# DeltaNet mixer of a two-layer decoder step: logits by float32 products in column groups, first decays spread by TensorE, gate and output products between the steps of the block inverse

## The chip, the cores and the metric

The kernel runs on one core of a Trainium2 chip. The metric is device time in microseconds of one execution. The core's engines run side by side and meet at semaphores: PE (TensorE, products into PSUM), DVE (VectorE), ACT (ScalarE), POOL (GpSimd) and SP (SyncE, which here issues the transfers).

## The reference, cut to what matters

Two macaron layers act on 544 tokens (a prompt of 512 and a sample group of 8 x 4) with 1024 channels. A layer is a feed-forward half step, a mixer, and another feed-forward half step. The change is in the mixer of the second layer, a gated DeltaNet with 8 heads of 128 channels:

```python
def deltanet_mixer(u, conv_buf, S0, w_in, conv_w, A_log, dt_bias, o_gain, w_out):
    proj = u @ w_in
    qkv, z, b_logit, a_logit = jnp.split(proj, [3 * DN_WIDTH, 4 * DN_WIDTH, 4 * DN_WIDTH + DN_HEADS], axis=-1)
    qkv, new_buf = causal_conv(conv_buf, qkv, conv_w)
    ...
    beta = jax.nn.sigmoid(b_logit.astype(jnp.float32))
    g = -jnp.exp(A_log.astype(jnp.float32)) * jax.nn.softplus(a_logit.astype(jnp.float32) + dt_bias.astype(jnp.float32))
    o, S = gated_delta_chunked(q, k, v, beta, g, S0)
    o = rms_norm(o, o_gain) * jax.nn.silu(z.reshape(B, T, DN_HEADS, DN_HEAD_DIM).astype(jnp.float32))
    return o.reshape(B, T, DN_WIDTH).astype(u.dtype) @ w_out, (new_buf, S)
...
def gated_delta_chunked(q, k, v, beta, g, S0):
    G = jnp.cumsum(gc, axis=-1)
    decay = jnp.exp(jnp.where(incl, G[..., :, None] - G[..., None, :], -jnp.inf))
    A = jnp.where(strict, jnp.einsum('bnhcd,bnhsd->bnhcs', kc, kc) * decay, 0.0) * bc[..., None]
    sol = lax.linalg.triangular_solve(A, rhs, left_side=True, lower=True, unit_diagonal=True)
    ...
    def step(S, xs):
        U = uv - jnp.einsum('bhcd,bhde->bhce', wk, S)
        O = jnp.einsum('bhcd,bhde->bhce', qq, S) + jnp.einsum('bhcs,bhse->bhce', p, U)
        S = gg[..., None, None] * S + jnp.einsum('bhcd,bhce->bhde', kk, U)
```

## The kernel before, in words

Tokens lie along the free dimension: each of the 8 tiles `x` holds 128 channels of all 544 tokens, in two halves of 256 and 288 columns. A large product (`mm3`, L371 to L373) keeps float32 accuracy by splitting both sides in a high and a low part (`xh`, `xl`; `wh`, `wl`) and multiplying three times per 128 channels: 24 matmuls for a half, 48 for a weight tile of 128 output channels, into PSUM buffers called `lin`. Its weights come by a DMA (`raw`), and ACT (L332) and DVE (L333) split them.

The mixer works on pairs of heads, called groups 0, 2, 4 and 6 by their first head. `ODD_ORDER` lists its pieces in the order in which they are written: D (decays of a pair), H (q and k of a head, convolution, k k^T and q k^T), B (values), V (the diagonal 32x32 blocks of the triangular solve, 31 small steps on DVE at L1257 and L1258, with transfers through DRAM that end in `V<-tdr`), L (`levels`, which builds the inverse of the 128x128 blocks from the 32x32 ones), S (the sample group), C (`chain`, the recurrence over four chunks, and `finish`, which normalizes and gates the outputs `y`), R (sample state), Z (gate of a head), O and M (output product of one group, or of groups 2 and 4 together), N (convolution state). Within this, a list scheduler sets the final order on every engine from its own estimates; each engine then runs its instructions strictly in that order.

`odd_setup` comes first: the 16 logits per token as an `mm3` product with a 16 columns wide weight (`lin` with 128\*16 weights in the trace), scaled by `rstd` into `bt` (L1049), turned by transposes (L1053), then beta, g, the cumulative sums `G` (L1076 to L1080), and its transpose `gt`, which goes to DRAM (`gdr`). A DMA spreads each head's row over all partitions (`grow` or `xsq`, and `grs` for the sample), and 8 DVE instructions a head (L1171, L1172) form the decays `Dn` and `Dt`.

In `levels` all small products (L1282 to L1309) use one PSUM slot, "c", and each step's result is evacuated by DVE and ACT before the next: transposes `pt`, `py`, `pz` (24 matmuls), a second `py`, a second `pz`. What the scheduler finds ready runs on PE between these steps. The `chain` of the last group calls `finish` after chunk 2 and after chunk 4, and the output product of group 6 takes the first half of the tokens first, in tiles of 6 matmuls.

The constants of the mixer are loaded by `odd_consts` at the start of the feed-forward step ahead of it, and `E.junk` is a tile that takes the unwanted output of ACT's squares.

## Time and profile before

| | |
|---|---|
| median of 3 runs | 1913.84 us (1910.95 to 1916.3) |
| the profiled execution | 1910.86 us, of which 1909.1 us from the first to the last instruction |
| mean granted clock of TensorE | 0.991 |
| PE, DVE, ACT busy | 97%, 57%, 44% of the span |
| the mixer, 1189 to 1610 us | PE 399.23, DVE 341.82, ACT 255.49 of 421.00 us, clock 0.97 |

The trace gives each instruction a start and a length; the idle time of its engine before it and what ended that idle time stand in brackets. Matmuls are pipelined, so the pace of a run of them is the distance of their starts. The granted clock of a window is a mean between the two levels of TensorE's clock, 1.2 GHz (0.50) and 2.4 GHz (1.00).

### The profile page before, as it was taken

To read this page: it belongs to the slowest core of one execution; us is meant where nothing else is said; L and a number is where in the kernel's file an instruction comes from. 1 tells how busy PE (TensorE), PEld (TensorE's weight loads), DVE (VectorE), ACT (ScalarE), POOL (GpSimd) and SP (SyncE) were. 2 spreads that over 40 slices of the span, in tenths; PEclk is the share of its full clock that TensorE was granted. 3 is DMA by queue.
4 is the path that set the end of the run, shared out by engine and by line. 5 is a ranking of instruction groups with operands and counts; after the bars stand their busy time and mean duration, and the time that the engine had idled before them with its cause. 6 is when DMAs were issued, how large, how long until landed. Compare 5 with 4: busy or idle time off the path is not lost.

```text
span 1909.1 us, 36695 instructions
## 1 busy us (share of the span) xinstructions
PE 1860.2 (97%) x15101; PEld 1790.8 (94%) x15101; DVE 1078.9 (57%) x2565; ACT 836.2 (44%) x1733; POOL 123.6 (6%) x229
## 2 busy tenths in 40 slices
PE   7999999999999999999999999999999998999999
PEld 6999999889778999999999999899888988999998
DVE  7444434786866444434444433898878867444422
ACT  6333224777755333323333322566675636333221
POOL 0000001111430000000000000212111100000000
PEclk8999999999999999999999999999999999999999
DMA  4333333312432333223333322334333332333242
GB/s 128 86 88 89 89 89 89 90 57 80 138 100 69 89 89 89 82 86 101 87 88 88 93 86 75 88 98 113 82 102 88 95 90 59 89 89 88 78 112 69
DMA packets 315973, 171.05 MB, mean 90 GB/s; under 512 B 28470, under 2 KB 310278, under 8 KB 315804
## 3 DMA queue, kind: packets, MB, share of 16 engines
q1 hardware_dynamic: 313244, 160.30, 29.6%
q0 software_dynamic: 2560, 8.39, 1.5%
q8 instruction: 119, 1.95, 0.4%
...
## 4 chain that ended last, share of the span: by engine, by line
PE 59%; DVE 4%; ACT 3%; DMA 1%; issue 1%; SPq 0%; ACTq 0%; DVEq 0%
PE lin L371 18%; PE lin L373 18%; PE lin L372 18%; PE m L1217 0%; DMA raw<-in_w_in_odd 0%; DMA raw<-in_w_ffn_in 0%; DVE acc L1140 0%; DVE wl L333 0%; DVE LT L1258 0%; PE c L1355 0%; PE c L1323 0%; DMA S<-in_state_dn_S 0%; DVE ltmp L1257 0%; PE c L1309 0%; PE c L1304 0%
## 5 line engine op out<-in xcount | busy, mean ns | idle before, releaser
L371 PE MATMUL lin<-xh,wh 128*128 128x256 f32 (+2 forms) x2992 | 873.0, 292 | 12.2 <-DVE x L1594 4.2
L372 PE MATMUL lin<-xl,wh 128*128 128x256 f32 (+2 forms) x2992 | 868.1, 290 | 0.7 <-DVE xl L273 0.6
L373 PE MATMUL lin<-xh,wl 128*128 128x256 f32 (+2 forms) x2992 | 865.6, 290 | 1.5 <-DVE wl L333 1.5
L371 PEld LDWEIGHTS lin<-xh,wh 128*128 128x128 f32 (+1 forms) x2992 | 563.9, 189 | 18.7 <-DVE x L1594 4.2
L373 PEld LDWEIGHTS lin<-xh,wl 128*128 128x128 f32 (+1 forms) x2992 | 565.3, 189 | 3.7 <-DVE wl L333 1.9
L372 PEld LDWEIGHTS lin<-xl,wh 128*128 128x128 f32 (+1 forms) x2992 | 564.2, 189 | 2.7 <-DVE xl L273 1.5
L332 ACT ACTIVATE wh<-raw 128x1024 fp32r<-128x1024 f32 x261 | 275.6, 1057 | 494.9 <-PE lin L372 429.4
L333 DVE TENSOR_TENSOR wl<-raw,wh 128x1024 fp32r<-128x1024 f32 x261 | 317.6, 1217 | 89.9 <-PE lin L373 88.0
L371 PE MATMUL lin<-hh,wh 128*128 128x288 f32 (+1 forms) x1024 | 295.7, 289 | 0.0
L372 PE MATMUL lin<-hl,wh 128*128 128x288 f32 (+1 forms) x1024 | 295.4, 288 | 0.0
L373 PE MATMUL lin<-hh,wl 128*128 128x288 f32 (+1 forms) x1024 | 294.9, 288 | 0.0
L372 PEld LDWEIGHTS lin<-hl,wh 128*128 128x128 f32 x1024 | 193.0, 188 | 0.2
L373 PEld LDWEIGHTS lin<-hh,wl 128*128 128x128 f32 x1024 | 192.7, 188 | 0.1
L371 PEld LDWEIGHTS lin<-hh,wh 128*128 128x128 f32 x1024 | 192.5, 188 | 0.1
L410 DVE TENSOR_TENSOR sg<-lin,rstd 128x256 f32<-128x256 f32 (+1 forms) x128 | 56.1, 438 | 162.5 <-PE lin L373 162.3
L415 DVE TENSOR_TENSOR pr<-lin,rstd 128x256 f32<-128x256 f32 (+1 forms) x128 | 56.5, 441 | 155.2 <-PE lin L373 155.2
L379 ACT ACTIVATE hh<-pr 128x256 fp32r<-128x256 f32 (+1 forms) x128 | 55.1, 431 | 202.8 <-DVE pr L416 202.6
L432 DVE SCALAR_TENSOR_TENSOR x<-lin,x 128x256 f32<-128x256 f32 x64 | 28.2, 441 | 168.4 <-PE lin L373 168.4
L380 DVE TENSOR_TENSOR hl<-pr,hh 128x256 fp32r<-128x256 f32 (+1 forms) x128 | 56.6, 442 | 61.2 <-ACT hh L379 61.2
L100 ACT ACTIVATE sg<-sg 128x256 f32<-128x256 f32 (+1 forms) x128 | 53.9, 422 | 56.1 <-DVE sg L410 56.1
L272 ACT ACTIVATE xh<-x,vec 128x544 fp32r<-128x544 f32 (+2 forms) x64 | 39.6, 632 | 71.8 <-DVE x L432 59.6
L1140 DVE SCALAR_TENSOR_TENSOR acc<-XP,cw,acc 128x568 f32<-128x568 f32 x72 | 58.7, 818 | 2.5 <-ACT acc L1138 1.8
...
## 6 DMA issues: line engine op xcount, KB each, us to landing
raw<-in_w_ffn_in SPq DMA_DIRECT2D x128, 512.0 KB
...
```

Of the source, the lines that this page charges most:

```text
L100: i = self.nc.scalar.activation(out, in_, func, **kw).ins
L272: nc.scalar.activation(xh, x, AF.Copy, scale=g)
L332: nc.scalar.activation(self.h, raw, AF.Copy)
L333: nc.vector.tensor_tensor(self.l, raw, self.h.bitcast(F32), op=ALU.subtract)
L371: nc.tensor.matmul(ps[:n], lhsT=wh, rhs=rh, start=(i == 0), stop=False)
L372: nc.tensor.matmul(ps[:n], lhsT=wh, rhs=rl, start=False, stop=False)
L373: E.last_mm = nc.tensor.matmul(ps[:n], lhsT=wl, rhs=rh, start=False, stop=(i == len(terms) - 1)).ins
L379: nc.scalar.activation(yh, src, AF.Copy)
L380: nc.vector.tensor_tensor(yl, src, yh.bitcast(F32), op=ALU.subtract)
L410: nc.vector.tensor_tensor(s, ps, E.rstd[:, c0:c0 + cn], op=ALU.mult)
L415: nc.vector.tensor_tensor(p_, ps, E.rstd[:, c0:c0 + cn], op=ALU.mult)
L1140: nc.vector.scalar_tensor_tensor(a, XP[:, j:j + XW - 3], cw[j], a, op0=ALU.mult, op1=ALU.add)
```

## The change

The logits. `odd_consts` now loads the 1024x16 logit weights into `bw`, zero-padded to 32 columns, and DVE multiplies them by the norm's gains, all at the start of the feed-forward step ahead of the mixer. `odd_setup` multiplies them with the raw float32 tiles `x`, in 16 matmuls that put four channel tiles in four groups of 32 output partitions; `rstd` scales the result, and a float32 product with `bsum` (four stacked identities) adds the groups where the transposes were. The logits have to follow the norm's own products (`E.norm_mm`). Three constants are loaded later, in `odd_setup`.

The first decays. For heads 0 and 1 and for the sample, matmuls with a broadcast column of the identity spread the rows of `gt` over all partitions into PSUM, and DVE reads them there; the other heads still use the DMA.

The fill. Gate products of heads 0 to 3, half of O0 and M2 in quarters leave `ODD_ORDER` and are called inside `levels`, one piece after each of its first four steps; each later step on PE has to stand behind the last matmul of the piece before it. M2 is then split in m-tiles 0 to 3 (fill) and 4 to 7. The four pieces of O0 cover all of it.

The unwanted squares go to `kt`, `vb` and `kw` in place of `junk`.

```diff
-ODD_ORDER = "D0 H0 H1 B0 B1 V0 Z0 L0 Z1 S0 C0 R0 D2 H2 B2 H3 B3 Z2 Z3 V2 L2 D4 S2 C2 R2 H4 H5 B5 D6 Z4 B4 V4 Z5 H6 S4 H7 B6 L4 V6 C4 R4 B7 Z6 O0 Z7 S6 N L6 C6 R6 M2 O6"
+ODD_ORDER = "D0 H0 H1 B0 B1 V0 L0 S0 C0 R0 D2 H2 B2 H3 B3 V2 L2 D4 S2 C2 R2 H4 H5 B5 D6 Z4 B4 V4 Z5 H6 S4 H7 B6 L4 V6 C4 R4 B7 Z6 Z7 S6 N L6 C6 R6 M2 O6"
+FILL = {0: ("Z00", "Z01", "Z10", "Z11"), 2: ("Z20", "Z21", "Z30", "Z31"), 4: ("O002", "O022", "O042", "O062"),
+        6: ("M201", "M211", "M221", "M231")}
...
+    E.bw = op.tile([P, KD, 32], F32, name="bw")
+    nc.vector.memset(E.bw, 0.0)
+    nc.sync.dma_start(out=E.bw[:, :, :16], in_=w_in[:, 4096:4112].rearrange("(k p) c -> p k c", p=P))
+    for k in range(KD):
+        nc.vector.tensor_scalar(E.bw[:, k], E.bw[:, k], col(E, "norm_mix", KD + k), None, op0=ALU.mult)
...
-    w = W(E, w_in[:, 4096:4112])
...
-    mm3(E, [w], E.xh, E.xl, ev)
+    for (c0, cn), tag in zip(HALVES, ("z", "pv")):
+        ps = cps(E, [P, cn], tag)
+        for i in range(2):
+            for j in range(4):
+                mm = nc.tensor.matmul(ps[32 * j:32 * j + 32], lhsT=E.bw[:, 4 * i + j], rhs=E.x[4 * i + j][:, c0:c0 + cn], start=(i == 0), stop=(i == 1), skip_group_check=True)
+                E.after(mm.ins, E.norm_mm)
+        nc.vector.tensor_tensor(bt[:, c0:c0 + cn], ps, E.rstd[:, c0:c0 + cn], op=ALU.mult)
...
-        nc.tensor.transpose(ps[:n, t], bt[:16, c0:c0 + n], E.ident[:16, :16])
+        nc.tensor.matmul(ps[:n, t], lhsT=bt[:, c0:c0 + n], rhs=E.bsum, start=True, stop=True)
...
-    nc.sync.dma_start(out=E.grs, in_=E.gdr[:, T:].unsqueeze(0).to_broadcast([P, NH, NS]))
+    row = lambda r: E.ident[:40, r:r + 1].to_broadcast([40, P])
+    ps = cps(E, [P, NH, NS], "s")
+    for h in range(NH):
+        nc.tensor.matmul(ps[:, h], lhsT=row(32 + h), rhs=gt[:40, :NS], start=True, stop=True)
+    nc.scalar.activation(E.grs, ps, AF.Copy)
+    E.growps = [cps(E, [P, 4, P], t) for t in ("c", "z")]
+    for h, ps in enumerate(E.growps):
+        for c in range(4):
+            nc.tensor.matmul(ps[:, c], lhsT=row(8 * c + h), rhs=gt[:40, :P], start=True, stop=True)
...
-    nc.sync.dma_start(out=grow, in_=E.gdr[h:h + 1].to_broadcast([P, NT]))
+    if h < GH:
+        src = E.growps[h]
+    else:
+        nc.sync.dma_start(out=grow, in_=E.gdr[h:h + 1].to_broadcast([P, NT]))
+        src = ch(grow)
...
-def levels(E, op, Hs, tdr):
+def levels(E, op, Hs, tdr, fill):
+    behind = []
+
+    def mm(*a, **kw):
+        i = nc.tensor.matmul(*a, **kw).ins
+        for b in behind:
+            E.after(i, b)
+
+    def full_products():
+
+        fill()
+        behind[:] = [E.last_mm]
...
     nc.scalar.activation(TN[64:96, :, :32], pt[64:96], AF.Copy)
+    full_products()
     py = cps(E, [P, n, 32])
...
+            fills = iter(FILL[i])
+
+            def fill():
+                for f in next(fills).split():
+                    k, j, m = f[0], int(f[1]), int(f[2])
+                    if k == "Z":
+                        gate(j, (m,))
+                    else:
+                        out(j, GH if k == "O" else 2 * GH, ms=range(m, m + int(f[3])))
+            H.V = levels(E, op, H.hs, H.tdr, fill)
```

PE at the start of the mixer. In the program before, the first rows are the norm's products (L288, L289) amid the logit products (`lin_13130`, second half); `bt` are the scaled logits.

```order
L288 MATMUL m_13079<-r_13074,onesr 128x256 [waits Activation_49]
...
L289 MATMUL m_13079<-r_13075,onesr 128x256 [waits DVE_49]
...
L289 MATMUL m_13089<-r_13075,onesr 128x288 [waits DVE_49]
...
L1053 MATMUL m_13156<-ident,bt_13103 128x16 [waits DVE_49]
L1053 MATMUL m_13156<-ident,bt_13103 128x16
```

In the changed program the product under the norm (`lin_13303`) is the q tile of head 0.

```order
L372 MATMUL lin_13303<-xl_938_6641,wh_13270 128x288
L289 MATMUL m_13096<-r_13082,onesr 128x288 [waits DVE_49]
L1060 MATMUL z_13105<-x_77,bw 32x256
L1060 MATMUL z_13105<-x_78,bw 32x256
...
L1060 MATMUL pv_13115<-x_84,bw 32x288
L373 MATMUL lin_13303<-xh_937_6640,wl_13271 128x288
...
L1069 MATMUL m_13129<-bsum,bt_13104 128x16 [waits DVE_49]
L1069 MATMUL m_13129<-bsum,bt_13104 128x16
```

The 48 logit products are gone, and the q tile, which stood behind the transposes, stands under the norm. Between the new logits and the first product with `bsum` there are four matmuls of the q tile.

PE in group 2, at the sample group's small steps, which invert its 32x32 blocks (L1436, L1443, L1447, L1461 before; L1481, L1488, L1492, L1505 after). Before, the large products `lin_16050` and `lin_16076` stand between the steps: 6 ahead of L1443, 11 ahead of L1447, 8 ahead of L1461 and 7 behind it.

```order
L1436 MATMUL s_15527<-ident,sA_15522 32x32 [waits DVE_49]
...
L372 MATMUL lin_16050<-xl_940_6643,wh_16043 128x256
L1443 MATMUL s_15535<-sA_15522,sB_15530 32x32 [waits DVE_49]
...
L373 MATMUL lin_16050<-xh_7_91,wl_16044 128x256
L371 MATMUL lin_16050<-xh_8_92,wh_16043 128x256
L1447 MATMUL s_15539<-sIB_15531,sA_1938_15532 32x32 [waits DVE_49]
...
L372 MATMUL lin_16050<-xl_16_100,wh_16043 128x256
...
L372 MATMUL lin_16076<-xl_938_6641,wh_16043 128x288
L1461 MATMUL s_15554<-sV_15542,skw_15544 128x32 [waits DVE_49]
...
L373 MATMUL lin_16076<-xh_937_6640,wl_16044 128x288
```

After, three large products stand ahead of L1488 and none from there past L1505; the others ran before L1481.

```order
L1481 MATMUL s_15518<-ident,sA_15513 32x32 [waits DVE_49]
L371 MATMUL lin_15926<-xh_8_92,wh_15893 128x288
L372 MATMUL lin_15926<-xl_16_100,wh_15893 128x288
L373 MATMUL lin_15926<-xh_8_92,wl_15894 128x288
L1488 MATMUL s_15526<-sA_15513,sB_15521 32x32 [waits DVE_49]
L1488 MATMUL s_15526<-sA_15513,sB_15521 32x32
L1492 MATMUL s_15530<-sIB_15522,sA_1940_15523 32x32 [waits DVE_49]
L1492 MATMUL s_15530<-sIB_15522,sA_1940_15523 32x32
L1505 MATMUL s_15544<-sV_15533,skw_15486 128x32 [waits DVE_49,Activation_49]
L1220 MATMUL m_15964<-ident,acc_15884 128x128 [waits Activation_49]
```

PE in the chain of group 6. Before, in the third chunk (`z`: U, `pv`: outputs, `c`: state), three products of M2 (`lin_18724`) stand between the chunk's output product and the state product that needs U.

```order
L1350 MATMUL z_18397<-S_18386,WT_18347 128x128 [waits DVE_49]
L1348 MATMUL z_18397<-vb_17760,V_18242 128x128
L1350 MATMUL z_18397<-S_18386,WT_18347 128x128 [waits DVE_49]
L1365 MATMUL pv_18410<-S_18386,qg_16857 128x128 [waits Activation_49]
L372 MATMUL lin_18724<-y_15487,wh_18678 128x288
L373 MATMUL lin_18724<-y_15486,wl_18679 128x288
L371 MATMUL lin_18724<-y_16867,wh_18678 128x288
L1355 MATMUL c_18404<-U_18402,kt_16808 128x128 [waits Activation_49]
L1366 MATMUL pv_18410<-U_18402,Dt_16351 128x128
L1365 MATMUL pv_18410<-S_18386,qg_17233 128x128
```

After, none does; neither is there one in the other chunks, since 154 of M2's 192 matmuls stand ahead of the first step of `levels` of this group and the other 38 between its steps. The next large product, `lin_18796`, is O6's first half.

```order
L1394 MATMUL z_18511<-S_18500,WT_18461 128x128 [waits DVE_49]
L1392 MATMUL z_18511<-vb_17890,V_18232 128x128
L1394 MATMUL z_18511<-S_18500,WT_18461 128x128 [waits DVE_49]
L1409 MATMUL pv_18524<-S_18500,qg_16847 128x128 [waits Activation_49]
L1399 MATMUL c_18518<-U_18516,kt_16789 128x128 [waits Activation_49]
L1410 MATMUL pv_18524<-U_18516,Dt_16341 128x128
L1409 MATMUL pv_18524<-S_18500,qg_17223 128x128
...
L1381 MATMUL c_18559<-ident,ot_18472 128x128 [waits DVE_49,Activation_49]
L371 MATMUL lin_18796<-xh_7_91,wh_18792 128x256 [waits Activation_49]
L1399 MATMUL c_18572<-U_18570,kt_16789 128x128 [waits DVE_49]
```

## Rows read from the trace of the kernel before

**Rows 1.** Windows: the mixer (columns in the first line), and 20 us inside it.

```profile
core 0: us, PE busy (x) PEld busy (x) DVE busy (x) ACT busy (x) POOL busy (x), PEclk, DMA share, GB/s
1189.00:1610.00 421.00, 399.23 (x3697) 370.54 (x3696) 341.82 (x1205) 255.49 (x738) 62.02 (x128) 0.97 0.34 90
1320.00:1340.00 20.00, 20.00 (x164) 19.45 (x163) 18.56 (x63) 18.80 (x66) 3.85 (x8) 1.00 0.56 156
```

**Rows 2.** Windows in which TensorE's clock fell, and the mixer's last stretch.

```profile
1196.00:1204.00 8.00, 6.00 (x38) 5.16 (x36) 4.74 (x15) 3.31 (x8) 0.95 (x1) 0.79 0.25 68
1360.00:1368.00 8.00, 8.00 (x43) 6.91 (x43) 4.51 (x18) 2.95 (x10) 0.25 (x2) 0.59 0.25 68
1396.00:1404.00 8.00, 8.00 (x48) 7.68 (x48) 5.17 (x13) 4.39 (x12) 1.68 (x3) 0.58 0.40 109
1560.00:1568.00 8.00, 6.11 (x36) 5.30 (x37) 5.83 (x18) 3.42 (x11) 0.00 (x0) 0.57 0.27 84
1590.00:1612.00 22.00, 17.51 (x126) 16.00 (x126) 20.64 (x51) 15.36 (x39) 0.00 (x0) 1.00 0.17 49
```

**Rows 3.** Timeline of PE: first, ninth and last logit product, a stall (start, length, instruction).

```profile
1189.18 0.28 PE L371 MATMUL lin<-xh,wh 128*16 128x256 f32 x1
...
1190.12 0.28 PE L373 MATMUL lin<-xh,wl 128*16 128x256 f32 x1
...
1196.89 0.29 PE L373 MATMUL lin<-xh,wl 128*16 128x288 f32 x1
...
1199.19 0.29 PE L1053 MATMUL m<-ident,bt 16*128 16x16 f32 x2 [2.00 <-DVE bt L1049]
```

**Rows 4.** Timeline of PE: runs of plain float32 products (records, two for each call).

```profile
1234.74 1.16 PE L1217 MATMUL m<-acc,acc 128*128 128x128 f32 x8
...
1469.55 1.94 PE L1485 MATMUL s<-S,wqz 128*32 128x128 f32 x60 [0.96 <-DMA S<-in_state_dn_S]
```

**Rows 5.** Timeline of PE and DVE: group 0's first decay and the stall behind the decays.

```profile
1220.38 0.33 DVE L1171 SCALAR_TENSOR_TENSOR Dn<-grow,G,c_mba 128x128 f32<-128x128 f32 x1
...
1225.23 0.37 PE L371 MATMUL lin<-xh,wh 128*128 128x288 f32 x1 [0.85 <-DVE XP L1130]
```

**Rows 6.** Timeline of DVE: the setup's last step to g; a step of group 2's sample group.

```profile
1207.75 0.20 DVE L1071 SCALAR_TENSOR_TENSOR g<-g,ad 128x40 f32<-128x40 f32 x1
...
1362.98 0.21 DVE L1444 COPY sA<-s 32x64 f32<-32x64 f32 x1 [0.47 <-PE s L1443]
```

**Rows 7.** Timeline of PE: stalls in group 2's levels.

```profile
1384.50 0.24 PE L1282 MATMUL c<-ident,V 32*32 32x32 f32 x2 [1.29 <-DMA V<-tdr]
...
1389.28 0.69 PE L1290 MATMUL c<-V,Dn 32*32 32x32 f32 x32 [0.28 <-ACT lv L1285]
...
1393.95 1.14 PE L1304 MATMUL c<-V,Dn 64*64 64x64 f32 x16 [0.42 <-DVE lv L1301]
```

**Rows 8.** Timeline of PE: stalls in group 6's levels.

```profile
1559.06 0.22 PE L1297 MATMUL c<-lv 32*32 32x32 f32 x2 [0.73 <-ACT lv L1292]
...
1560.36 0.51 PE L1526 MATMUL s<-um,k 96*128 96x512 f32 x1 [0.60 <-ACT um L1524]
...
1562.40 1.96 PE L1304 MATMUL c<-V,Dn 64*64 64x64 f32 x16 [1.53 <-DVE lv L1301]
```

**Rows 9.** Timeline of PE and DVE: end of group 6's chain, its first y, O6.

```profile
1581.62 0.49 PE L1366 MATMUL pv<-U,Dt 128*128 128x128 f32 x2
...
1586.01 0.43 DVE L380 TENSOR_TENSOR xl<-sz,xh 128x256 fp32r<-128x256 f32 x1
...
1595.24 0.39 PE L371 MATMUL lin<-xh,wh 128*128 128x256 f32 x1 [1.31 <-DVE x L1594]
```

**Rows 10.** `V<-tdr` by tile; where the load and scaling of `bw` come.

```profile
L1276 SPq DMA_DIRECT2D V<-tdr x4: 342/444/452, 1379.5 to 1380.8; - x4
...
901.09 0.42 SPq L1008 DMA_DIRECT2D c_smba<-in_c_smba  x1
...
904.78 0.46 DVE L296 SCALAR_TENSOR_TENSOR rstd<-xsq,f 128x288 f32<-128x288 f32 x1
```

More of the change, by code (lines that the diff above doesn't have):

```diff
@@ L288, in rsqrt_half @@
     nc.tensor.matmul(ps, lhsT=ones, rhs=sh, start=True, stop=False)
-    nc.tensor.matmul(ps, lhsT=ones, rhs=sl, start=False, stop=True)
+    E.norm_mm = nc.tensor.matmul(ps, lhsT=ones, rhs=sl, start=False, stop=True).ins
     E.act(y, ps, AF.Ln, bias=E.eps, scale=1.0 / width)
@@ L1000, in bc, with odd_consts @@
     return ap.unsqueeze(2).to_broadcast([ap.shape[0], ap.shape[1], n])
-def odd_consts(E, op):
+def odd_consts(E, op, w_in):
     nc, I = E.nc, E.I
@@ L1017, in odd_consts @@
     E.bsel = const("c_bsel", [96, DB])
+    E.bw = op.tile([P, KD, 32], F32, name="bw")
[3 more added lines that the diff above has]
+        nc.vector.tensor_scalar(E.bw[:, k], E.bw[:, k], col(E, "norm_mix", KD + k), None, op0=ALU.mult)
+    E.bsum = op.tile([P, 16], F32, name="bsum")
+    nc.vector.tensor_tensor(E.bsum, E.ident[:, 0:16], E.ident[:, 32:48], op=ALU.add)
+    for j in (2, 3):
+        nc.vector.tensor_tensor(E.bsum, E.bsum, E.ident[:, 32 * j:32 * j + 16], op=ALU.add)
     rows = E.f(P)[:96]
@@ L1187, in head_stage @@
     ssk = op.tile([P, 4], F32, tag="ssk", name=E.nm("ssk"), bufs=2)
+    kt = op.tile([P, 4, P], F32, tag="st", name=E.nm("kt"), bufs=ST)
     pq = E.m([P, 4, P])
@@ L1191, in head_stage @@
     for c in range(4):
-        nc.scalar.activation(E.junk[0], pq[:, c], AF.Square, accum_out=ssq[:, gi, c:c + 1])
-    kt = op.tile([P, 4, P], F32, tag="st", name=E.nm("kt"), bufs=ST)
+        nc.scalar.activation(kt[:, c], pq[:, c], AF.Square, accum_out=ssq[:, gi, c:c + 1])
     pk = E.m([P, 4, P])
@@ L1281, in levels @@
             s = slice(32 * i, 32 * i + 32)
-            nc.tensor.matmul(pt[s, x], lhsT=V[s, x, s], rhs=E.ident[s, s], start=True, stop=True, tile_position=(32 * i, 32 * i))
+            mm(pt[s, x], lhsT=V[s, x, s], rhs=E.ident[s, s], start=True, stop=True, tile_position=(32 * i, 32 * i))
     nc.vector.tensor_copy(TN[0:32, :, :32], pt[0:32])
@@ L1289, in levels @@
             f, s = slice(64 * b, 64 * b + 32), slice(64 * b + 32, 64 * b + 64)
-            nc.tensor.matmul(py[f, x], lhsT=A[s, c, f], rhs=V[s, x, s], start=True, stop=True, tile_position=(64 * b + 32, 64 * b))
+            mm(py[f, x], lhsT=A[s, c, f], rhs=V[s, x, s], start=True, stop=True, tile_position=(64 * b + 32, 64 * b))
     nc.vector.tensor_copy(Y[0:32, :, :32], py[0:32])
     nc.scalar.activation(Y[64:96, :, :32], py[64:96], AF.Copy)
+    full_products()
     pz = cps(E, [P, n, 64])
@@ L1537, in odd_mixer @@
         E.ft, E.rt = (op, "acc", XW, 4), (op, "y", YB)
-        E.junk = [op.tile([P, P], F32, name=f"junk{i}") for i in range(2)]
         norm_stats(E)
@@ L1561, in head, with gate @@
         head_stage(E, op, w_in, h, H.hs[h % GH], H.ssq, H.adr, H.sq)
-    def gate(h):
+    def gate(h, halves=(0, 1)):
         H = st[h // GH * GH]
         E.table("silu_and_others")
-        z = op.tile([P, NT], F32, tag="sz", name=E.nm("sz"), bufs=3)
-        H.sz = getattr(H, "sz", []) + [z]
-        w = W(E, w_in[:, 3072 + h * P:3072 + (h + 1) * P])
+        if 0 in halves:
+            z = op.tile([P, NT], F32, tag="sz", name=E.nm("sz"), bufs=3)
+            H.sz = getattr(H, "sz", []) + [z]
+            H.zw = W(E, w_in[:, 3072 + h * P:3072 + (h + 1) * P])
+        z = H.sz[h % GH]
         def ev(hf, c0, cn, ps):
@@ L1584, in y_tiles, with out @@
         return [Y[g0 + h] for h in range(GH)]
-    def out(g0, n, halves=((0, 1),), last=False):
+    wide_out = {}
+    def out(g0, n, halves=((0, 1),), last=False, ms=range(KD)):
         yh = {g: Y[g][0] for g in range(g0, g0 + n)}
         yl = {g: Y[g][1] for g in range(g0, g0 + n)}
-        ws = wide(E, w_out, list(range(g0, g0 + n)))
+        if g0 not in wide_out:
+            wide_out[g0] = wide(E, w_out, list(range(g0, g0 + n)))
+        ws = wide_out[g0]
         step = KD if n <= GH or len(halves) == 1 else 16 // n
-        for m, hs in [(m, hs) for m0 in range(0, KD, step) for hs in halves for m in range(m0, m0 + step)]:
+        for m, hs in [(m, hs) for m0 in range(0, KD, step) for hs in halves for m in range(m0, m0 + step) if m in ms]:
             def ev(h, c0, cn, ps):
@@ L1627, in odd_heads @@
         elif c == "L":
-            H.V = levels(E, op, H.hs, H.tdr)
+            fills = iter(FILL[i])
[7 more added lines that the diff above has]
+            H.V = levels(E, op, H.hs, H.tdr, fill)
         elif c == "C":
@@ L1635, in odd_heads @@
                 out(i, GH, ((0,), (1,)), True)
-            else:
+            elif i not in wide_out:
                 out(i, GH)
@@ L1640, in odd_heads @@
         elif c == "M":
-            out(i, 2 * GH)
+            out(i, 2 * GH, ms=range(4, KD))
         elif c == "N":
```

43 lines of the change are left out of this document (22 added, 21 removed).

## Prediction

> **What bounds the kernel now.** I read the windows by stage first: the mixer takes 421 us, PE is busy for 399 of them, and its clock is 0.97 [rows 1]. In the twenty microseconds shown DVE is busy 18.6 of 20 beside it, so there both are near their limit [rows 1]. What the change can win is PE's idle time, its time at half clock, and work taken off it. The narrower windows show four places where the clock falls [rows 2]: behind the setup (0.79 over 8 us), and in group 2 (twice) and group 6 (0.57 to 0.59). At full pace a window of 8 us at clock c loses 8 x (1 - c): 1.7, 3.3, 3.4 and 3.4 us, 11.8 in all. The timeline of PE then shows what stands ahead of each: 2.00 us without work at the transposes of the logits [rows 3], stalls among the small products of levels [rows 7, 8]. The last stretch, O6, is DVE's: 20.64 of 22 us busy [rows 2].
>
> **The setup.** Removed are 48 logit products. They start 0.1175 us apart (eight steps in 0.94 us, rows 3; the wider half costs 288/256 of it), so 24 x 0.1175 + 24 x 0.132 = 6.0 us. They also wait for `xh` and the norm, but the q tile of head 0 has the same inputs and takes the same place, so those waits stay and I count only the work. The 2.00 us for `bt` [rows 3] should be covered, since 48 q products stand under the norm and four behind the new logits; with it goes the half clock behind it, 1.7 us [rows 2]. The stall of 0.85 us behind group 0's decays [rows 5] stood behind 16 DVE instructions, one each 0.26 us, that waited for a DMA; they now read PSUM. Removed: 6.0 + 2.0 + 1.7 + 0.85 = 10.55 us.
>
> Added are 16 logit calls, 32 records. No row shows this shape. The product with 32-column weights runs 60 records in 1.94 us, 0.032 each; the full-width one 8 records in 1.16 us, or 0.126 each without the last one's own 0.28 [rows 4]. With twice the columns, if the four groups run side by side, 32 x 0.032 x 2.1 = 2.2 us; one after another 32 x 0.126 x 2.1 = 8.5. I take 2.2: the row with 32 columns is the same form. The sums through `bsum` cost some 0.2 more than the transposes (between 0 and 5 calls at 0.25). The spread is 8 calls of 128 columns, 16 x 0.126 = 2.0 us, and 8 of 32 columns, between 16 x 0.032 = 0.5 and 2.0, say 1.0. Then g: before, it was ready 8.8 us after the first transposes (1207.95 less 1199.19, rows 3 and 6), behind the evacuations of the q tile and a weight split on DVE; PE now reaches the cumulative sums sooner, and I let it wait 1.2 us, between none and the 2.00 of the old stall. Added: 2.2 + 0.2 + 3.0 + 1.2 = 6.6. The setup gives 10.55 - 6.6 = 4.0 us, which DVE also gets: it starts the first convolutions that much earlier.
>
> The scaling of `bw` is hidden, if its load is in time. In the order it is the sixth of SP's loads there, where `c_smba` is issued now, at 901.09; DVE needs it ahead of its row at 904.78, the second half's `rstd` [rows 10]; behind that stand the evacuations of the first products, and PE's next free buffer. The nearest row is `V<-tdr`: issues from 1379.5 to 1380.8, landed by 1384.5 [rows 7, 10], so 3.7 to 5.0 us. That is 0 to 1.3 us late on DVE, and PE has no stall there now; I take 0, and 3 us as the far end. The squares that go to `kt`, `vb`, `kw` cost the same ACT instructions; their new waits are for tiles free long before: 0, with 1 us as the far end.
>
> **The sample group of group 2.** Before, 6, 11 and 8 large products stood between its four small steps; after, 3 and none. Each step waits for one small DVE instruction: that took 0.21 us and had waited 0.47 us for PE [rows 6], so a round trip is about 0.7 and PE stands still some 0.47 in each. Three to four such steps: 1.4 us lost (none if DVE's other work makes them wait anyway as before, 2.7 if each costs 0.7).
>
> **Levels of group 2.** Ten large products now stand between `pt` and `py`, and ten before the last step, where there were one and six. The stalls of 0.28 and 0.42 [rows 7] go: -0.7. The 1.29 for `V<-tdr` stays, since the fill comes behind that step. The window from 1396 at 0.58 [rows 2] came right behind the second of them. If it goes with them, that is 3.4 us more. I think it likelier than not that one of the two in group 2 goes, and count it: -3.4; the ends are 0 and -6.7.
>
> The fill adds changes between full and small tiles, about ten in the mixer. The full-width row and the small one stand beside each other in levels now already, and no idle is put down to it [rows 7]; I count 0. The Trainium skill, "TensorEngine Tiling (Array Packing)", section Key Properties, says that changing the tiling mode drains TensorE. No row here shows a drain as such; by that rule ten changes at a tenth of a microsecond each (my estimate) would make the sum 1 us worse.
>
> **Groups 0 and 4.** Group 0's gates were done ahead of its levels before, and are after. In group 4 large products filled the steps before, too, and its largest wait nearby, 0.96 us, is for the sample state's DMA [rows 4], which no fill shortens: 0.
>
> **Group 6 and the tail.** Its levels lost 0.73 + 0.60 + 1.53 = 2.9 us [rows 8] and 3.4 to half clock [rows 2]; the 38 products left of M2 cover the first, so both go: -6.3. But M2 is spent then. Before, 22 of its matmuls lay in the chain under the waits for U; they made the chain no longer, and after, that time is idle: 22 x 0.125 = 2.8 us come back, as the work has to stand elsewhere. Behind the chain, PE had M2 until 1590; the first gated `y` was ready at 1586.4, 4.5 us after the chain's last U product at 1581.62 [rows 9]. Some 1.3 us of that holds other products, so 3.2 us of idle come back. Sum: -6.3 + 2.8 + 3.2 = -0.3. O6 itself stays DVE's [rows 2], with the same work and stalls like the 1.31 us for `x` [rows 9].
>
> **The sum.** -4.0 + 1.4 - 0.7 - 3.4 - 0.3 = -7.0. Against the profiled execution's own 1910.86 us this is 1903.9; that run is at the low end of the three shown, and against their median, 1913.84, it is 1906.8.
>
> **The rivals.** What a measurement of this kernel can tell from no change is about 0.3%, 5.7 us.
> - *The setup alone.* The half clock in group 2 stays or moves: -3.6 us, 1910.2. For it: levels of group 2 still has two state products and 24 small ones in a row, without fill. Against it: the stalls ahead go.
> - *DVE takes the gain.* It is busy 18.6 of 20 us where PE is never idle [rows 1]. The 4 us are won only if DVE, too, starts earlier; if its queue, not PE's, sets groups 0 to 4, 1 to 3 us are left: about 1912.
> - *The tail runs at half clock (slower).* The chain has no large product left, and PE idles until the first `y`. Half clock followed such gaps in group 6's levels [rows 8, 2]. If it falls in the chain and stays through O6, the chain's 10.5 us of PE work take up to 6 us more, and O6's tiles of six, 0.71 to 0.80 us now, take 1.4 to 1.6 and pass DVE's 1.25 (20.64 us for 16 tiles, less some), 16 x 0.25 = 4: +10 against a rest of -7.0, so +3; with group 2's stretch kept +6.4, 1920. It decides when the granted clock is at 0.5 from the chain to O6's end. Against it: before, the clock was 1.00 in O6 with PE busy 17.5 of 22 [rows 2].
> - *The load of `bw` is late*: its 1024 pieces of 64 bytes hold DVE, and then PE, at the feed-forward step's start: +3 on any case. For it speaks only that it is the load of the smallest pieces. The Trainium skill, "DMA: Bandwidth & Descriptors", table at its head, says that pieces under 512 B do not reach line rate; no run here shows this load. By that rule this rival gains; at twice the 5.0 us of the nearest row [rows 7, 10] DVE would be 6 us late and PE about 3.
>
> **Chances.** The forecast (setup and at least one stretch of group 2): 0.42, between 1900 and 1908. The setup alone, 0.22; DVE takes the gain or `bw` is late, 0.18; the slower tail, or more than one cost at its far end, 0.18. So faster 0.42, same 0.39, slower 0.19. The range has to reach from both stretches gone (-10.4, 1903.4, less 2 for costs at their low ends) to the slower tail at 1919.
>
> **What would show it.** Right: in the setup, 16 logit calls within 2.5 us, no stall over 0.5 us at the first `bsum` product, and a clock of 1.00 there; in group 2's levels no stall from `lv`; in group 6, no stall from `lv`, and idle of 0.3 to 0.5 us in each chunk of the chain, then some 3 us before O6. Wrong: logits near 8 us (groups one after another), a wait of over 2 us at the cumulative sums, a clock of 0.5 in the chain or in O6, a stall of PE near 905 us, or stalls of the same total in groups 2 and 4 for DVE's evacuations.

## The result, and the profile after

The changed kernel is slower: 1922.8 us (median of 8 runs, 1919.84 to 1927.97) beside 1914.14 us for the kernel before (8 runs, 1906.78 to 1916.54) on the same chip; ratio 1.0057, 95% interval 1.0044 to 1.0070, so about 11 us (the medians lie 8.7 us apart). The forecast was 1906.8, with 1901 to 1919 as its range: the time lies outside.

The windows of the changed kernel, by stage, come first. The window runs from 1180 to 1640 us in every kernel, and the cuts are landmarks on PE: the first transpose of each group's levels (`c<-ident,V`) and its first `c<-V,kw` product. So the ten rows are the setup, then levels and the rest for groups 0, 2, 4 and 6, then the norm.

```profile
core 0: us, PE busy (x) PEld busy (x) DVE busy (x) ACT busy (x) POOL busy (x), PEclk, DMA share, GB/s
1180.00:1297.01 117.01, 114.24 (x917) 108.73 (x917) 96.17 (x322) 66.41 (x172) 21.94 (x53) 1.00 0.32 83
1297.01:1312.91 15.90, 14.81 (x279) 12.92 (x278) 6.97 (x18) 7.84 (x23) 2.67 (x6) 1.00 0.50 129
1312.91:1385.35 72.44, 69.18 (x539) 66.26 (x537) 64.44 (x251) 47.90 (x149) 14.40 (x27) 0.95 0.33 87
1385.35:1400.72 15.37, 14.44 (x277) 12.57 (x277) 6.45 (x15) 10.46 (x35) 2.80 (x4) 1.00 0.49 127
1400.72:1476.84 76.12, 70.57 (x577) 67.22 (x576) 63.03 (x251) 47.91 (x147) 12.11 (x27) 0.93 0.37 95
1476.84:1505.81 28.97, 25.66 (x290) 23.77 (x290) 21.23 (x68) 13.60 (x44) 1.66 (x3) 0.82 0.21 56
1505.81:1568.16 62.35, 58.22 (x505) 53.65 (x503) 42.69 (x160) 28.32 (x81) 5.76 (x8) 1.00 0.39 106
1568.16:1582.42 14.26, 13.26 (x219) 11.14 (x217) 11.32 (x41) 9.24 (x29) 0.39 (x1) 1.00 0.08 23
1582.42:1624.28 41.86, 36.20 (x239) 32.73 (x240) 30.56 (x96) 25.53 (x75) 0.00 (x0) 0.92 0.17 49
1624.28:1640.00 15.72, 13.56 (x107) 13.16 (x106) 8.70 (x19) 8.79 (x16) 0.00 (x0) 1.00 0.34 99
```

A stage's length less PE's busy time is PE's idle time in it. The same landmarks cut in the other traces give this table (idle time of PE in us, worked out so from their windows, with the measured ratio; L0 is the levels of group 0, rest 0 what follows up to the levels of the next group; the kernels are told in the next section):

| kernel | setup | L0 | rest 0 | L2 | rest 2 | L4 | rest 4 | L6 | rest 6 | norm | sum | ratio |
|---|---|---|---|---|---|---|---|---|---|---|---|---|
| before | 5.9 | 0.6 | 3.1 | 0.7 | 3.1 | 0.3 | 0.4 | 3.0 | 4.7 | 0.3 | 22.0 | 1 |
| after | 2.8 | 1.1 | 3.3 | 0.9 | 5.6 | 3.3 | 4.1 | 1.0 | 5.7 | 2.2 | 29.9 | 1.0057 |
| squares_alone | 5.8 | 0.0 | 3.3 | 1.5 | 7.3 | 0.6 | 6.0 | 1.0 | 4.1 | 0.4 | 29.9 | 1.0040 |
| junk_back | 2.9 | 0.0 | 5.6 | 0.9 | 2.2 | 1.7 | 1.0 | 1.1 | 4.1 | 2.1 | 21.6 | 0.9994 |
| setup_junk | 3.2 | 0.0 | 6.4 | 1.2 | 2.4 | 0.3 | 0.4 | 2.6 | 4.7 | 2.1 | 23.3 | 1.0000 |
| no_fill4_junk | 2.8 | 0.0 | 5.6 | 0.6 | 2.4 | 0.2 | 0.6 | 0.9 | 4.0 | 2.1 | 19.2 | 0.9966 |
| kt_squares_alone | 6.0 | 0.0 | 4.0 | 0.0 | 12.6 | 0.0 | 2.8 | 1.3 | 5.9 | 0.2 | 32.9 | 1.0054 |
| vb_squares_alone | 5.7 | 0.6 | 3.1 | 0.7 | 2.5 | 0.4 | 1.0 | 0.0 | 4.6 | 0.2 | 18.8 | 0.9966 |

The first two lines are the story of the change: the setup won its 3 us, and the stages of groups 2 and 4 lost 9.2 (2.5, 3.0 and 3.7). PE's timeline in the setup, which answers to [rows 3], shows the win:

```profile
1193.95 1.07 PE L1060 MATMUL z<-x,bw 128*32 128x256 f32 x16
1194.83 1.15 PE L1060 MATMUL pv<-x,bw 128*32 128x288 f32 x16
1196.60 0.62 PE L1069 MATMUL m<-bsum,bt 128*128 128x16 f32 x4
...
1213.98 1.97 PE L1131 MATMUL s<-gt,ident 40*128 40x32 f32 x16
1215.79 1.14 PE L1136 MATMUL c<-gt,ident 40*128 40x128 f32 x8
1216.76 1.05 PE L1136 MATMUL z<-gt,ident 40*128 40x128 f32 x8
```

Both halves of the logits take 1194.83 + 1.15 - 1193.95 = 2.03 us, and the first `bsum` product waits for nothing.

Group 2's stage lost its time around the finish of its chain. PE, then DVE:

```profile
1423.21 0.33 PE L1381 MATMUL c<-ident,ot 128*128 128x128 f32 x1 [1.88 <-ACT ot L1378]
...
1431.05 0.58 PE L371 MATMUL lin<-xh,wh 128*128 128x256 f32 x1 [2.63 <-DVE sz L1616]
```

```profile
1422.29 0.35 DVE L1200 SCALAR_TENSOR_TENSOR Dn<-xsq,G,c_mba 128x128 f32<-128x128 f32 x1 [2.46 <-DMA xsq<-gdr]
...
1430.58 0.41 DVE L1616 TENSOR_TENSOR sz<-lin,rstd 128x256 f32<-128x256 f32 x1
```

PE had finished gate 5's product and wanted a `lin` buffer. DVE empties it into one of three `sz` buffers, and that one is free only when the finish has used it: the finish itself waited, since `fo` (its factor) stood on DVE behind 2.46 us for a transfer. Group 4's levels have one large stall, and the clock of that stage is 0.82. PE, then DVE:

```profile
1482.75 0.58 PE L371 MATMUL lin<-y,wh 128*128 128x256 f32 x1 [3.27 <-DVE x L1643]
```

```profile
1479.12 0.80 DVE L1165 SCALAR_TENSOR_TENSOR acc<-XP,cw,acc 128x568 f32<-128x568 f32 x1
...
1482.29 0.77 DVE L1643 TENSOR_TENSOR x<-lin,x 128x256 f32<-128x256 f32 x2
```

This is the fill O0: tiles of 6 matmuls, which PE makes faster than DVE, busy with convolution steps, can empty them. In the rest of group 4 the largest stall is for the sample group's state:

```profile
1566.27 1.94 PE L1529 MATMUL s<-S,wqz 128*32 128x128 f32 x60 [1.71 <-DMA S<-in_state_dn_S]
```

In the kernel before, this product of group 6's sample group waits for nothing (1547.39 us).

### The profile page after: what moved, and what is told of

Same layout as the page of the kernel before. It is cut to its first block, busy times and chain, and to the rows that moved or that the text cites. A ratio compares the mean times of both kernels' runs of the same rounds, so it can differ in the third digit from the quotient of the medians.

```text
span 1920.2 us, 36736 instructions
## 1 busy us (share of the span) xinstructions
PE 1863.4 (97%) x15122; PEld 1795.5 (94%) x15122; DVE 1076.2 (56%) x2576; ACT 832.7 (43%) x1733; POOL 123.2 (6%) x229
## 4 chain that ended last, share of the span: by engine, by line
PE 59%; DVE 6%; ACT 2%; DMA 1%; issue 1%; SPq 0%; DVEq 0%; ACTq 0%
PE lin L371 18%; PE lin L372 17%; PE lin L373 17%; DVE acc L1165 1%; PE c L1301 1%; DVE wl L333 1%; DVE LT L1287 1%; DVE ltmp L1286 1%; PE s L1529 0%; DMA raw<-in_w_in_odd 0%; PE c L1399 0%; PE pv L1410 0%; PE c L1367 0%; DMA xsq<-gdr 0%; DMA S<-in_state_dn_S 0%
## 5 line engine op out<-in xcount | busy, mean ns | idle before, releaser
L371 PE MATMUL lin<-xh,wh 128*128 128x256 f32 (+1 forms) x2976 | 870.0, 293 | 14.6 <-DVE sg L410 3.5
L372 PE MATMUL lin<-xl,wh 128*128 128x256 f32 (+1 forms) x2976 | 866.1, 291 | 0.6 <-DVE xl L273 0.6
L373 PE MATMUL lin<-xh,wl 128*128 128x256 f32 (+1 forms) x2976 | 862.1, 290 | 1.4 <-DVE wl L333 1.4
L371 PEld LDWEIGHTS lin<-xh,wh 128*128 128x128 f32 x2976 | 564.3, 190 | 19.1 <-DVE x L1643 4.3
L373 PEld LDWEIGHTS lin<-xh,wl 128*128 128x128 f32 x2976 | 565.5, 190 | 3.3 <-DVE wl L333 1.8
L372 PEld LDWEIGHTS lin<-xl,wh 128*128 128x128 f32 x2976 | 564.7, 190 | 3.8 <-issue 1.8
L416 DVE TENSOR_TENSOR pr<-pr,sg 128x256 f32<-128x256 f32 (+1 forms) x128 | 56.0, 438 | 6.4
```

Of the source, the lines that this page charges most:

```text
L371: nc.tensor.matmul(ps[:n], lhsT=wh, rhs=rh, start=(i == 0), stop=False)
L372: nc.tensor.matmul(ps[:n], lhsT=wh, rhs=rl, start=False, stop=False)
L373: E.last_mm = nc.tensor.matmul(ps[:n], lhsT=wl, rhs=rh, start=False, stop=(i == len(terms) - 1)).ins
L416: nc.vector.tensor_tensor(p_, p_, sg[:, c0:c0 + cn], op=ALU.mult)
```

## The experiments

All ratios are to the kernel before, on the same chip. Theories are named in the quoted expectations as they stood then; what each stood for is told here.

**Which half costs the time?** The first theory was the fill: more products between the steps push DVE's and ACT's work back. `setup_alone` keeps the new logits, decays and squares, with the order of before and no fill; `fill_alone` the reverse, with the new squares too.

```diff
# setup_alone, against the changed kernel
-ODD_ORDER = "D0 H0 H1 B0 B1 V0 L0 S0 ...
-FILL = {0: ("Z00", ...
+ODD_ORDER = "D0 H0 H1 B0 B1 V0 Z0 L0 Z1 S0 ...
+FILL = {}
```

> The changed kernel's setup, decays and squares, with the order of the kernel before and no fill inside levels. Theory A (the losses come from the fill: 7.9 us at 1420 to 1440, 6.9 at 1480 to 1500, 4.4 behind 1540; the setup itself wins 4.5 us of idle and half clock and 0.8 of work): faster than the kernel before by 4 to 6 us, ratio 0.997. Theory B (the setup's shift upsets the order in groups 2 and 4, the fill is innocent): slower than before, ratio 1.003 or more.

> The kernel before's setup and decays by DMA, with the changed order and the fill inside levels. Theory A: slower than the changed kernel itself by about 5 us, ratio to before 1.008. Theory B: the losses at 1420 and 1480 are absent, ratio 1.002 or less.

Measured: 1.0047 [1.0031, 1.0063] and 1.0050 [1.0030, 1.0069]. Each half alone is as slow as the whole, and neither theory holds: A asked for 0.997 from `setup_alone`, B for 1.002 or less from `fill_alone`. The fill is not the whole cause.

**Single places.** `o0_out_of_levels` takes O0 out of group 4's levels (`Z6 O0 Z7` in the order, no entry 4 in `FILL`); `gate5_later` writes gate 5 behind head 6 (`V4 H6 Z5 S4`).

> The changed kernel without fill in group 4: O0 stands in the order where it stood before. Theory A (the six-matmul tiles of O0 outrun DVE's evacuations behind three convolution steps, 3.27 us, and 4.5 us of half clock follow): 6 to 7 us faster than the changed kernel, ratio to before 1.002, and no half clock at 1480 to 1492. Rival (O0's evacuations cost PE the same wherever they stand, since DVE is the bound): within 2 us of the changed kernel.

> The changed kernel with the gate of head 5 written after head 6, so that its products come behind the chain of group 2 and a tile of head 5 stands where they stood. Theory A (the gate's evacuation waits for one of the three gate buffers, which comes free only with the gated output of group 2; PE stands 2.63 us and runs at half clock behind it): the 2.63 goes, 4 to 6 us faster than the changed kernel, ratio to before 1.003. Rival (the wait of DVE for the decay row's DMA, 2.46 us, is the cause, and the late outputs of group 2 with it): the 1.88 us and the half clock stay, less than 2 us faster.

Measured: 1.0036 [1.0022, 1.0051] and 1.0060 [1.0037, 1.0083]. O0's stall went (idle of that stage 0.6), but the loss behind the levels of groups 2 and 4 stayed (5.9 and 6.0 us of idle). With gate 5 written later the loss stayed as well, though not at the same instructions: of the stalls of 1.88 and 2.63 us only 0.72 us of the first is left, and in their place PE waits 1.56 us for DVE's `XP` and 1.94 us for a state of the sample group, so the stage keeps 5.3 us. Gate 5's place in the written order was not the cause. The same O0 pieces cost only 0.9 us of idle in group 4's levels there: what they cost depends on what DVE has to do beside them.

**What both halves share** is the squares. `junk_back` is the changed kernel with the two junk tiles; `squares_alone` is the kernel before with nothing but the squares moved; `setup_junk` is `setup_alone` with the junk tiles; `no_fill4_junk` is `o0_out_of_levels` with them.

```diff
# squares_alone, against the kernel before
+    kt = op.tile([P, 4, P], F32, tag="st", name=E.nm("kt"), bufs=ST)
...
-        nc.scalar.activation(E.junk[0], pq[:, c], AF.Square, accum_out=ssq[:, gi, c:c + 1])
-    kt = op.tile([P, 4, P], F32, tag="st", name=E.nm("kt"), bufs=ST)
+        nc.scalar.activation(kt[:, c], pq[:, c], AF.Square, accum_out=ssq[:, gi, c:c + 1])
...
-        nc.scalar.activation(E.junk[0], pk[:, c], AF.Square, accum_out=ssk[:, c:c + 1])
+        nc.scalar.activation(kt[:, c], pk[:, c], AF.Square, accum_out=ssk[:, c:c + 1])
...
-            nc.scalar.activation(E.junk[1], ot[:, c, h], AF.Square, accum_out=sso[:, h, c:c + 1])
+            nc.scalar.activation(Hs[h].vb[:, c], ot[:, c, h], AF.Square, accum_out=sso[:, h, c:c + 1])
...
```

> The changed kernel with the two junk tiles back as the targets of ACT's squares. So far both halves of the change apart, setup alone and fill alone, were 0.5% slower, as slow as the whole; what both have in common is that squares go to kt, vb and kw. Theory C (these targets cost the time: idle of PE in groups 2 and 4 behind the levels, 2.5 and 3.6 us more in every kernel that has them): the loss goes, ratio to before at most 1.001. Theory D (every change of the written order reshuffles the list scheduler's result, and the order before was a lucky one): stays at 1.003 to 1.006.

> The kernel before with ACT's squares written to kt, vb and kw and without the junk tiles, and nothing else. Theory C: slower by 6 us or more, ratio 1.003 to 1.006. Theory D: also slower, if the order moves as much; told apart from C by the place, which under C is ACT's squares waiting for those tiles, under D other instructions.

> Setup and first decays changed, junk tiles kept, order of before, no fill. Theory C: the setup's 4 to 5 us are won, ratio 0.997 to 0.998. Theory D: 1.002 to 1.005.

> The changed kernel with junk tiles back and O0 out of group 4's levels. Theory C: 6 us better than the same kernel without junk tiles (1.0036), so 1.000 to 1.001. Theory D: 1.002 to 1.005.

Measured: 0.9994 [0.9981, 1.0006], 1.0040 [1.0024, 1.0056], 1.0000 [0.9988, 1.0012] and 0.9966 [0.9953, 0.9979]. The squares alone, in the old kernel, bring most of the loss, and at the same places; PE in `squares_alone`:

```profile
1434.84 0.33 PE L1337 MATMUL c<-ident,ot 128*128 128x128 f32 x1 [1.57 <-ACT ot L1334]
...
1441.62 0.39 PE L371 MATMUL lin<-xh,wh 128*128 128x256 f32 x1 [2.64 <-DVE sz L1570]
```

They answer to the 1.88 and 2.63 us of the changed kernel. `setup_junk` missed: 0.997 to 0.998 was expected, and it wins nothing (see below). On one chip, `junk_back` and `no_fill4_junk` differ by O0's place alone: 0.28%, some 5 us, for the fill of group 4; the two intervals just don't overlap. Idle time shows 2.4 us of it, with a stall of 1.11 us for DVE's `x` among O0's tiles; the rest is not located.

**Which squares?** `kt_squares_alone` and `vb_squares_alone` move one kind each in the kernel before; `kt_back` is the changed kernel with only the squares of q and k back on one junk tile. `m2_held` is `no_fill4_junk` with m-tiles 4 to 7 of M2 held behind group 6's first transposes, so that the chain has large products again.

> The kernel before, with only the squares of q and k written to kt. Theory C1 (kt comes from the pool of 15 tiles shared with Dn, Dt, qg and vb; its buffer is needed from the first square of q on, not from the evacuation of k on, and must first be given up by the chain and by the transfers that read Dn of the group before; so head 3, 5 and 7 move 16 to 30 us later): this alone brings the loss, ratio to before 1.003 to 1.005, and the squares of heads 3, 5 and 7 begin some 20 us later than before. Rival C2 (vb as target holds vb longer): 1.000 here.

> The kernel before, with only the squares of the outputs written to vb. Theory C1: within 0.1% of before, heads 3, 5 and 7 where they were. Rival C2: ratio 1.003 to 1.005.

> The changed kernel with one junk tile back, as the target of the squares of q and k alone; vb and kw stay targets. Theory C1: as with both junk tiles back, 0.999 to 1.000. Rival C2: 1.003 or more.

> Junk tiles back, O0 out of group 4's levels, and half of M2 (m-tiles 4 to 7) held on PE behind the transposes of group 6's levels, so that 96 of its products cover levels, chain and finish. If M2's early end costs what the prediction took (idle in the chain and ahead of O6): 2 to 4 us faster than without the hold (0.9966), ratio 0.995. Rival (the tail is DVE's, and M2's evacuations then stand in it): same or slower, 0.9966 to 0.998.

Measured: 1.0054 [1.0037, 1.0071], 0.9966 [0.9954, 0.9978], 1.0014 [0.9998, 1.0029] and 0.9963 [0.9947, 0.9978]. `kt` is what costs. The seven kernels with squares on `kt` lie at 1.0036 to 1.0060, the nine without at 0.9958 to 1.0014. In `kt_squares_alone` PE waits at the same steps, the finish's transposes and the next large product:

```profile
1439.05 1.35 PE L1337 MATMUL c<-ident,ot 128*128 128x128 f32 x4 [3.57 <-ACT ot L1334]
...
1444.35 0.58 PE L371 MATMUL lin<-xh,wh 128*128 128x256 f32 x1 [1.92 <-DVE sz L1571]
```

The wait for the sample state ahead of group 6's product is there in all seven (1.2 to 2.1 us), and in none of the others. Squares on `vb` cost nothing; they win 0.34%, where no change was expected (within 0.1%), and at a place where they aren't: group 6's levels, whose idle goes from 3.0 to 0.0 us. No wait for `vb` explains that; it looks like a shift of the scheduler's order, so such a shift alone can be worth some 0.3%. The effects don't add up to the tenth: `kt` and `vb` alone give 0.20% together, `squares_alone` 0.40%, and `kt_back` lies 0.20% above `junk_back`, within the noise. The squares on `kw` were never moved by themselves. M2's place is worth nothing measurable beside `no_fill4_junk`.

The mechanism stands on ACT. First the kernel before, head 3: its first square of q, its evacuation of k; then the changed one: its first square, the output of group 0's last chunk, its evacuation of k.

```profile
1301.57 0.26 ACT L1192 ACTIVATE junk<-m 128x128 f32<-128x128 f32 x1
...
1328.41 0.59 ACT L1199 ACTIVATE kt<-m 128x512 f32<-128x512 f32 x1
```

```profile
1324.42 0.26 ACT L1222 ACTIVATE kt<-m 128x128 f32<-128x128 f32 x1
...
1325.99 0.38 ACT L1411 ACTIVATE ot<-pv 128x256 f32<-128x256 f32 x1
...
1327.87 0.60 ACT L1228 ACTIVATE kt<-m 128x512 f32<-128x512 f32 x1
```

`kt` comes from the tag "st", whose 15 buffers serve `Dn`, `Dt`, `qg`, `kt` and `vb` of three heads. Head 3 evacuates k into its `kt` at 1328 us in both. Its buffer comes free only near the end of group 0's chain: in the changed program it held `qg` of head 0, which the chain reads in every chunk. Before, the evacuation was the first write, and nothing hurried it; the squares had run 27 us earlier, and with them the factors of q and k that all later steps of the head need. After, the square is the first write. For heads 5 and 7 the buffer held `Dn` of heads 3 and 5, which transfers read, and the levels of groups 2 and 4 up to their second `py`. In the changed kernel each first square comes just behind that last reading, head 3's on PE at 1323.69, head 7's at 1496.58 us; ahead of head 7's square ACT stands idle for it:

```profile
1323.69 0.39 PE L1409 MATMUL pv<-S,qg 128*128 128x128 f32 x2
...
1496.58 1.14 PE L1301 MATMUL c<-V,Dn 64*64 64x64 f32 x16
...
1497.76 0.28 ACT L1222 ACTIVATE kt<-m 128x128 f32<-128x128 f32 x1 [1.53 <-PE c L1301]
```

The order of ACT shows the wait also for head 5, first before, then after; the wait for a transfer (`DMAHW7`) has moved from the evacuation to the square:

```
1120 L1199 ACTIVATE kt_2043_16193<-m_2044_16194 128x512 [waits DMAHW7_49,DMAHW0_49]

1116 L1222 ACTIVATE kt_2043_16174,ssq_1911_15432<-m_2044_16175 128x128 [waits DMAHW7_49]
```

In the traces, the first square of heads 3, 5 and 7 starts at 1301.6, 1380.0 and 1472.2 us before, and at 1324.4, 1396.6 and 1497.8 after: 17 to 26 us later. Heads 2, 4 and 6 keep their places. It is the same in all of the kernels with squares on `kt`, and in none of those with the squares of q and k on junk. The way from the late squares to PE's stalls is not followed step by step: it runs through the orders that the list scheduler makes of the late work, and `gate5_later` shows that the stalls can move.

**Where did the setup's gain go?** `setup_junk` is worth 0, though its setup idles 2.7 us less. Its table line shows 6.4 us behind group 0's levels instead of 3.1, and 2.1 at the norm instead of 0.3. Of the 6.4 the largest part is a stall of 3.06 us behind gate 3, whose second half stands on PE ahead of the finish. `gate3_half_held` is `setup_junk` with that half held behind the finish's transposes; `best_gate3_held` and `best_vb_held` do the same to `no_fill4_junk`, the second with squares of the outputs on `vb`.

```diff
# gate3_half_held, in gate(): E.turned is the last transpose of the finish, mm3 sets its first matmul behind E.hold
-        mm3(E, [H.zw], E.xh, E.xl, ev, halves=halves)
+        for hf in halves:
+            E.hold = E.turned if (h, hf) == (3, 1) else None
+            mm3(E, [H.zw], E.xh, E.xl, ev, halves=(hf,))
...
```

> setup_junk (new logits, new decays, both junk tiles, old order) with one edit: the second half of gate 3's product (24 matmuls) is held on PE behind the transposes of group 0's finish; all work is done. In setup_junk those 24 matmuls stood ahead of the finish, and the next q tile then waited 3.06 us for the evacuation of gate 3's first half, which DVE does only behind the finish. Theory G (the setup's 3 us were given back there): the finish starts 24 x 0.125 = 3.0 us earlier, the stall of 3.06 us falls under 0.7, the idle of the stage from group 0's first kw product to group 2's levels falls from 6.5 to about 3.5 us, and the ratio goes from 1.0000 to about 0.9984. Rival H (DVE or ACT sets the pace of that stage): the idle comes back at the sample group's steps or at the next convolution's evacuations, the stage keeps 5.5 us or more, and the ratio stays within 0.9992 to 1.0008.

> no_fill4_junk (all of the change but both junk tiles kept and O0 left out of group 4's levels; 0.9966) with the same hold on gate 3's second half; all work is done. Theory G: its stall of 3.18 us in group 0's finish goes too, and the ratio is about 0.9966 less 0.0016, 0.9950. Rival H: 0.9966 again.

> best_gate3_held with the output's squares on vb (one junk tile is left, for the q and k squares); all work is done. What won 0.34% in vb_squares_alone was by its trace the stalls in group 6's levels (idle 3.0 us there before, 0.0 with it, and 2.9 us at half clock that are gone). Theory I (it won that and no more): the fill of group 6 has taken the same stalls here, so the ratio stays that of best_gate3_held within 0.0010. Rival J (the squares on junk cost something of their own on ACT, wherever they stand): another 0.002 to 0.003 faster.

Measured: 0.9977 [0.9964, 0.9990], 0.9972 [0.9959, 0.9985] and 0.9958 [0.9943, 0.9973]. PE in `setup_junk`, then PE and ACT in `gate3_half_held`:

```profile
1353.94 0.58 PE L371 MATMUL lin<-xh,wh 128*128 128x256 f32 x1 [3.06 <-DVE sz L1616]
```

```profile
1348.88 1.36 PE L1384 MATMUL c<-ident,ot 128*128 128x128 f32 x4 [3.07 <-ACT ot L1381]
...
1348.42 1.28 ACT L1381 ACTIVATE ot<-ot,fo 128x128 f32<-128x128 f32 x4 [1.79 <-DVE fo L1000]
```

The stall didn't go: it moved from behind gate 3 to ahead of the finish, and the stage keeps 6.1 us of idle. Counted from group 0's first `c<-V,kw` product (1327.72 and 1328.70 us), PE comes to the finish's transposes 2.5 us earlier with the half held, and they start 20.2 us behind it instead of 19.9. So the finish is not late because PE comes late; DVE and ACT, which make its factor `fo` and use it, set its time. That is rival H by its mechanism, though the ratio came out as theory G said or better. The faster ratio is not from this stage: group 6's levels lost their stalls again (2.6 to 0.3 us) and their half clock (0.82 to 1.00), as with `vb_squares_alone`. In `best_gate3_held` nothing was won beyond `no_fill4_junk`, where G had said 0.9950. `best_vb_held` has the lowest ratio measured, but its interval overlaps those of `best_gate3_held`, `no_fill4_junk` and `m2_held`; between I and J, at 0.0014, it doesn't decide.

## Why the prediction was wrong

**The step that failed** is the sentence that closes the setup: the new waits of the squares "are for tiles free long before: 0, with 1 us as the far end". `kt` isn't free long before. It measured 0.54% alone (`kt_squares_alone`, 10 us) and 0.43% within the change (1.0057 less 1.0014, 8 us). I looked at the cost of the instructions and not at which event frees the buffer that they now write. With the squares on `vb` and `kw` back on junk as well, the difference is 0.63%, 12 us (1.0057 less 0.9994).

**Groups 0 and 4: 0.** Wrong for group 4. The pieces of O0 there are what the prediction listed as a sign of being wrong, stalls for DVE's evacuations: 3.27 us in one place, and 0.28% between `junk_back` and `no_fill4_junk`. I had seen that large products lay there before, but not that the pieces are tiles of 6 matmuls, whose pace DVE sets, as in O6 [rows 2]. The pieces are also all of O0, 96 matmuls, and not half of it, as the first sentence on the fill has it.

**The setup, -4.0.** The terms were close. Logits 2.2 us forecast, 2.03 measured, so the groups run side by side as in the nearest row [rows 4]; the spread 3.0, and 1213.98 to 1217.81 is 3.8, as the calls of 32 columns took 1.8 and not 1.0; the wait for g 1.2, none seen; the clock from 1197 to 1205 is 1.00, where 1196 to 1204 had 0.79 [rows 2]. Group 0's first `c<-V,kw` product starts at 1312.91 and started at 1317.02: 4.1 us. But it is not time won: `setup_junk` measured 1.0000. That is the rival "DVE takes the gain", with ACT beside DVE, at group 0's finish. The norm at the mixer's end also waits 1.8 us more (2.1 for 0.3) in all kernels with the new setup. The traces show what differs there: DVE and ACT split a weight ahead of the norm's first half (DVE at 1624.12, ACT at 1627.05 us), where before they did so behind it (1615.22 and 1617.59). ACT, first before, then after:

```profile
1616.74 0.42 ACT L294 ACTIVATE xsq<-f 128x256 f32<-128x256 f32 x1
1617.59 1.06 ACT L332 ACTIVATE wh<-raw 128x1024 fp32r<-128x1024 f32 x1 [0.44 <-DMA raw<-in_w_ffn_in]
```

```profile
1627.05 1.06 ACT L332 ACTIVATE wh<-raw 128x1024 fp32r<-128x1024 f32 x1
1628.02 0.40 ACT L294 ACTIVATE xsq<-f 128x256 f32<-128x256 f32 x1
```

The two splits take 1.23 and 1.06 us, about as much as the 2.16 us that PE waits for an evacuation that needs the norm. Why the scheduler turned the order there stays open.

**The sample group of group 2, +1.4.** In its range: PE stands still 0.78, 0.31 and 0.93 us ahead of three of the small steps (L1481, L1492 and L1505), 2.0 in all. But the stage's idle is 3.3 us beside 3.1, since other stalls went, the 1.29 for `V<-tdr` [rows 7] among them, which the prediction let stay.

**Levels of group 2, -0.7 and -3.4.** Idle is 0.9 instead of 0.7, since another stall of 0.94 us came in between two steps: nothing won. The clock of that stage is 1.00 instead of 0.85, which would be some 2.8 us of its 18.5 and most of the 3.4, but it can't be put down to the fill: `setup_alone` and `setup_junk`, without fill, have 1.00 too, and `kt_back`, with it, 0.68.

**Group 6, -6.3 +2.8 +3.2.** The stalls went as forecast, 3.0 to 1.0 us, and the clock came to 1.00 from 0.82. That is not shown to be the fill's doing: `setup_alone`, `squares_alone`, `kt_squares_alone`, `vb_squares_alone` and `gate3_half_held`, without fill, have 0.0 to 1.3 us and 1.00 there too. Of the 6.0 us said to come back, the table shows 1.0 (4.7 to 5.7; the 3.2 ahead of O6 rest on 4.5 us between two rows that are 4.8 apart). `m2_held`, which gives the chain large products again, changes idle and clock of the tail (5.3 us and 1.00, beside 4.0 and 0.92 in `no_fill4_junk`), and the time is the same within the noise: PE's time in the tail seems to cost little, as it would if DVE set its pace; no run shows that by itself. PE's rows in the changed kernel's chain and tail, which answer to [rows 9]:

```profile
1589.54 0.71 PE L1399 MATMUL c<-U,kt 128*128 128x128 f32 x4 [0.25 <-ACT U L1396]
1592.39 0.71 PE L1399 MATMUL c<-U,kt 128*128 128x128 f32 x4 [0.35 <-ACT U L1396]
...
1597.06 0.41 PE L1381 MATMUL c<-ident,ot 128*128 128x128 f32 x2 [0.67 <-DVE sz L1385]
...
1603.65 0.39 PE L371 MATMUL lin<-xh,wh 128*128 128x256 f32 x1 [1.17 <-DVE x L1643]
```

The idle of 0.3 per chunk was right; of the 3 us ahead of O6, 0.67 came. The half clock of the slower rival came only in part: 1590 to 1612 us ran at 0.98, but 1582 to 1590 at 0.79 and 1612 to 1618 at 0.78, and the whole tail at 0.92, where it had 1.00 before: some 3 us by the lengths of the two windows.

**The load of `bw`, 0.** Right: it was issued at 901.4 us, DVE scaled from 905.38 without a wait for it, and PE was busy 19.77 of 20 us from 895. The Trainium skill, "DMA: Bandwidth & Descriptors", table at its head, gives pieces under 512 B less than line rate; here the load of 64-byte pieces took no more than 4.0 us, inside the 3.7 to 5.0 of `V<-tdr`, which I had taken for it.

**The sum.** With both zeros taken out, `no_fill4_junk` measured -0.34%, 6.5 us, beside -7.0 forecast. That is no proof of its terms: the setup alone gives 0, and much of the rest lies in group 6's levels, where other edits of the order win the same, so it is luck that the sum came out near. What stays open is why the order there shifts so easily; no run holds it by itself.
